# A Strassen-split GLA layer on one core: evictions and scan steps ranked first, TensorE in source order

## The chip, the cores and the metric

The kernel runs on one NeuronCore of a Trainium2 chip. The metric is the time of one execution in microseconds of the device. Each core has five engines that run their own instruction streams side by side: TensorE (PE, matrix products), VectorE (DVE), ScalarE (ACT), GpSimd (POOL) and SyncE (SP, here only a queue that issues DMAs). An engine takes its instructions strictly in the order of its stream, so one that waits holds up all behind it.

## The reference

The program computes one layer: an RMS norm, a gated linear attention mixer (GLA), a residual add, another norm, a feed-forward block with a causal convolution, a residual add and a final norm. The sequence has 2048 rows, the model 1024 columns, all float32. Cut to what matters:

```python
h = rmsnorm(x, mix_norm_w)
proj = h @ w_in                      # q, k, v, r, glr
log_a = log_sigmoid(glr @ w_gate2 + b_gate) / 16
g = cumsum(log_a, within chunks of 64);  g_end = g[:, :, -1]
k_dec = k * exp(g_end - g)
for each chunk:                      # lax.scan over 32 chunks
    state = state * exp(g_end) + k_dec.T @ v
    o = q @ state
y = (rms_normalize(o) * norm_w * silu(r)) @ w_out
x = x + y
h = rmsnorm(x, ffn_norm_w)
u = causal_dwconv(h @ w_up, conv_w, conv_b);  g, val = split(u)
x = x + (silu(g) * val) @ w_down
return rmsnorm(x, final_norm_w)
```

## The kernel before

**Products.** Every large matrix product is computed to float32 accuracy from two reduced parts of each operand: `split(hi, lo, src)` makes the rounded part on ACT (a cast, L193) and the rest on DVE (a subtraction, L194). `mm3p` (L181 to L187) then issues three matmuls for each of four k slices: L184 takes the low part of the weight, L185 the low part of the row operand, L186 both high parts. On top of that a Strassen-like scheme computes a pair of row tiles by a pair of column blocks with seven products instead of eight, in the order `PORD` = p1, p5, p6, p2, p7, p3, p4, so each product is 12 matmuls of 128x512. A product leaves its sum in an accumulator bank in PSUM; p6, p7 and p4 add onto p1's bank and p3 onto p5's. Between two products that share a bank the sum so far must be copied out: this is an eviction. It is `cp1`, `cp5`, `cp6` on ACT (L1211), `o11`, `o22`, `o12` on DVE (`out`, L1154), `o21` on ACT (L1227), in the last projection the additions to the residual `x1` on DVE (L1199), and in the feed-forward block `c1`, `c2` on ACT (`copied`, L1297). The next product on the bank waits for it.

**Phases.** Four phases R, A, B, Y of eight units j (one unit is a pair of row tiles e = 2j, d = 2j+1, in `unit`): R projects r and the gates, A and B project q, k, v of two heads each and run the scan, Y is the output projection with the residual add. Then U is the up projection of the feed-forward block with its convolution (`phase_u`, by row half s and column block f) and D the down projection. Each phase loads raw weights (`wr_...`) into a ring of slots, splits them into `w_...` and frees the slots; rows (`hr_...`) are loaded, split into `h_...`.

**Scan.** For each of 32 tiles n (16 of A, 16 of B) there are four steps, put in between the matmuls of the products by `scan_slot`: `scan_f` (decay `kd` and its split `kz`, transposes `pq`, gate rows `r` loaded by DMA and passed through silu on ACT, L714), `scan_k` (products `pk`, the running `state` on DVE, splits `sh` and `sl`), `scan_o` (products `po`, sums of squares, `og` on DVE, with `rstd` from POOL), `scan_x` (transposes `px` of `og`, copies `ot`). The table `SLOTS` says behind which k slice of a unit each one stands.

**Gates.** Block b of four row tiles has `sums(tt)`: two matmuls `pd` (L639) of the split logarithms `lh`, `ll`, an exponential on ACT into `e` (L640), and `totals`: four transposes `pe` of `e` (L631), whose last columns ACT copies to `dec` (L633). Blocks 0 to 2 fall in R, block 3 at the start of A. A table load (`ACT_TABLE_LOAD`) stands on ACT wherever exp and silu follow one another.

**Order.** The source issues the instructions in one long list, with delayed work (`later_do`) taken up at due times. `scan_b`, which runs in unit 0 of A after p3, calls `need` on all gates, so that in the source all of block 3's `pd` and `pe` stand ahead of p4 of that unit. A scheduler then sets the order on each engine: of the instructions that it takes as ready it picks the one earliest in the source. So before, PE too may run a later product ahead of a step that is not ready by the scheduler's reckoning.

## Time and profile before

| what | us |
|---|---|
| median of three runs (2118.75 to 2119.75) | 2118.95 |
| profiled execution | 2119.17 |
| its span | 2117.5 |
| PE busy in the span | 2049.1 |
| DVE, ACT, POOL busy | 1605.2, 1109.4, 672.5 |
| phases on PE: R, A, B, Y | to 220, 429, 643, 831 |
| phases on PE: U, D | to 1690, 2109 |

The span is what the trace covers; 1.67 us lie around it. A row of the profile gives a start in us from the span's start, a duration, engine, source line, output, inputs and shape; in square brackets is the idle time of the engine ahead of the row and what ended it. The trace's rows leave out the numbers in names (`mp_A` is any product's bank in A, `h_A_p` any row operand). "PEclk" is the granted clock of TensorE as a share of full speed.

### The profile page before, as it was taken

How to read it: one execution, taken by the hardware profiler on the slowest of the kernel's cores; microseconds unless marked ns; L12 is line 12 of the kernel's file. 1: busy time of each engine (PE TensorE's matmuls, PEld its weight loads, DVE VectorE, ACT ScalarE, POOL GpSimd, SP SyncE). 2: the span in 40 equal slices, each digit the busy share in tenths (PEclk: the TensorE clock that was granted, in tenths of full speed). 3: DMA queues.
4: the chain of work that ended last, by engine and by line, in shares of the span. 5: the costliest groups of instructions: out<-in, count | busy, mean ns of one | idle time of the engine just before them, and what ended most of it. 6: DMA issues, size and time to landing. Idle time of an engine off the chain costs nothing.

```text
span 2117.5 us, 28200 instructions
## 1 busy us (share of the span) xinstructions
PE 2049.1 (97%) x9700; PEld 1686.1 (80%) x9700; DVE 1605.2 (76%) x2109; ACT 1109.4 (52%) x2022; POOL 672.5 (32%) x595
## 2 busy tenths in 40 slices
PE   6999999999998998999999999999999999999998
PEld 4777778878886887888888887888888788888886
DVE  7766887888878646899898867898898956566564
ACT  5656755675665666655545545445454533233342
POOL 2110000000000002555464554666766433243310
PEclk9999999999999999999999999999999999999999
DMA  8866675577858888444545376545445684454462
GB/s 293 295 219 199 223 237 178 165 247 254 292 183 267 314 271 293 155 159 136 182 139 167 132 278 204 140 110 152 122 129 148 196 322 155 144 179 164 148 218 112
DMA packets 246512, 419.32 MB, mean 198 GB/s; under 512 B 22784, under 2 KB 91520, under 8 KB 246368
## 3 DMA queue, kind: packets, MB, share of 16 engines
q1 hardware_dynamic: 203200, 335.09, 46.5%
q10 hardware_dynamic: 36832, 70.89, 9.8%
q0 software_dynamic: 6336, 11.54, 3.5%
q8 instruction: 76, 1.25, 0.2%
q14 instruction: 68, 0.56, 0.1%
HBM read 278.50 MB, written 150.47 MB: 203 GB/s over the span
## 4 chain that ended last, share of the span: by engine, by line
PE 64%; DVE 13%; POOL 7%; issue 7%; DMA 7%; ACT 2%; SPq 0%; ACTq 0%; DVEq 0%; POOLq 0%
PE pd_p L184 7%; PE pd_p L186 7%; PE pd_p L185 7%; DVE t L1315 4%; PE ua L185 4%; PE ua L184 4%; PE ua L186 3%; POOL as_p L1344 3%; DVE uw_p L194 3%; PE mp_A L184 2%; PE mp_Y L184 2%; PE mp_Y L185 2%; PE mp_Y L186 2%; PE mp_A L185 2%; PE mp_A L186 2%
## 5 line engine op out<-in xcount | busy, mean ns | idle before, releaser
L184 PE MATMUL ua<-h_p,uw_p 128*128 128x512 f32 x704 | 276.9, 393 | 10.2 <-ACT c L1297 4.5
L185 PE MATMUL ua<-h_p,uw_p 128*128 128x512 f32 x704 | 276.0, 392 | 2.8 <-DVE var_d L226 2.8
L186 PE MATMUL ua<-h_p,uw_p 128*128 128x512 f32 x704 | 275.5, 391 | 0.0
L1315 DVE SCALAR_TENSOR_TENSOR t<-u,cw,t 128x1024 f32<-128x1024 f32 x176 | 265.6, 1512 | 8.5 <-ACT t L1313 7.8
L184 PE MATMUL pd_p<-dw_p,da 128*128 128x512 f32 x616 | 239.6, 389 | 0.0
L185 PE MATMUL pd_p<-dw_p,da 128*128 128x512 f32 x616 | 239.6, 389 | 0.0
L186 PE MATMUL pd_p<-dw_p,da 128*128 128x512 f32 x616 | 239.6, 389 | 0.0
L193 ACT CAST uw_p<-us 128x512 fp32r<-128x512 f32 x132 | 82.2, 622 | 198.8 <-POOL us L1277 138.3
L194 DVE TENSOR_TENSOR da<-da_p,da 128x512 fp32r<-128x512 f32 x154 | 118.9, 826 | 87.9 <-ACT da L193 87.9
L194 DVE TENSOR_TENSOR uw_p<-us,uw_p 128x512 fp32r<-128x512 f32 x132 | 153.3, 1166 | 42.4 <-ACT uw_p L193 37.7
L194 DVE TENSOR_TENSOR uw_p<-ur,uw_p 128x512 fp32r<-128x512 f32 x176 | 146.3, 860 | 28.1 <-ACT uw_p L193 28.1
L184 PEld LDWEIGHTS ua<-h_p,uw_p 128*128 128x128 f32 x704 | 133.0, 189 | 43.2 <-ACT c L1297 8.9
L193 ACT CAST da<-da_p 128x512 fp32r<-128x512 f32 x154 | 84.7, 618 | 150.4 <-PE pd_p L186 115.3
L185 PEld LDWEIGHTS ua<-h_p,uw_p 128*128 128x128 f32 x704 | 133.0, 189 | 30.6 <-DVE uw_p L194 3.4
L186 PEld LDWEIGHTS ua<-h_p,uw_p 128*128 128x128 f32 x704 | 133.2, 189 | 27.9
L760 POOL TENSOR_TENSOR rstd<-var,pair 128x2 f32<-128x2 f32 x32 | 22.7, 709 | 410.7 <-DVE var L759 410.7
L184 PE MATMUL uc<-h_p,uw_p 128*128 128x512 f32 x352 | 137.1, 390 | 1.2 <-DMA h_p<-hd_p 1.2
L186 PE MATMUL uc<-h_p,uw_p 128*128 128x512 f32 x352 | 137.0, 389 | 0.0
L185 PE MATMUL uc<-h_p,uw_p 128*128 128x512 f32 x352 | 136.9, 389 | 0.0
L1313 ACT ACTIVATE t<-u,cw 128x1024 f32<-128x1024 f32 x88 | 109.6, 1245 | 49.9 <-DVE u L1424 49.1
L186 PEld LDWEIGHTS pd_p<-dw_p,da 128*128 128x128 f32 x616 | 115.6, 188 | 24.1
L185 PEld LDWEIGHTS pd_p<-dw_p,da 128*128 128x128 f32 x616 | 115.6, 188 | 24.1
(263 smaller groups left out, 5287.3 us busy)
## 6 DMA issues: line engine op xcount, KB each, us to landing
ur<-in_ffn_w_up_dram SPq DMA_DIRECT2D x84, 512.0 KB, 5.2
da_p<-ad_p SPq DMA_DIRECT2D x154, 256.0 KB, 4.1
ad_p<-t SPq DMA_DIRECT2D x110, 256.0 KB, 3.1
ch<-in_ffn_w_down_dram SPq DMA_DIRECT2D x61, 256.0 KB, 4.9
hr_A_p<-h1d_p SPq DMA_DIRECT2D x56, 256.0 KB, 3.3
hr_B_p<-h1d_p SPq DMA_DIRECT2D x56, 256.0 KB, 3.2
hr_Y_p<-yd_p SPq DMA_DIRECT2D x56, 256.0 KB, 3.9
hd_p<-h2p_p ACTq DMA_DIRECT2D x56, 256.0 KB, 2.1
```

What stands on the lines that cost most here:

```text
L184: nc.tensor.matmul(ps_ap, ah, bl, start=(first and i == 0), stop=False, **kw)
L185: nc.tensor.matmul(ps_ap, al, bh, start=False, stop=False, **kw)
L186: nc.tensor.matmul(ps_ap, ah, bh, start=False, stop=(last and i == len(pairs) - 1), **kw)
L193: order["act"] = nc.scalar.copy(hi, src)
L194: nc.vector.tensor_sub(lo, src, f32(hi))
L760: nc.gpsimd.tensor_tensor(rstd, var, neghalf.to_broadcast([P, 2]), op=ALU.pow)
L1313: nc.scalar.activation(t, u[:, 2:2 + TS], AF.Identity, scale=cw[:, 2, c:c + 1], bias=cw[:, 3, c:c + 1])
L1315: nc.vector.scalar_tensor_tensor(t, u[:, k:k + TS], cw[:, k, c:c + 1], t, op0=ALU.mult, op1=ALU.add)
L1344: upool["ins"] = nc.gpsimd.tensor_add(av, last if x is None else x, y)
```

## The change

It does three things. `manual_schedule(engines={PE})` makes TensorE keep the order in which the source issues its instructions. `high_priority(600)` ranks the evictions, and `high_priority(400)` the steps `scan_o`, `scan_k` and `scan_x` (not `scan_f`), as though they stood that many places earlier in the source, on the engines that the scheduler still orders. `ROWS` is not used. No instruction's shape or data changes; ACT gets 14 table loads in place of 12.

```diff
+    ctx.enter_context(tc.manual_schedule(engines={mybir.EngineType.PE}))
...
+    def first(n):
+        return tc.high_priority(n)
+    EVICT, SCAN, ROWS = 600, 400, 200
...
         def scan_slot(m):
             if ps_ == "Y" and j < 2:
                 for fn, n in SLOTS_END.get(28 * j + m, ()):
-                    fn(2 * NTT + n)
+                    with ExitStack() if fn is scan_f else first(SCAN):
+                        fn(2 * NTT + n)
             if ps_ in "AB":
                 for fn, n in SLOTS.get(m, ()):
-                    fn(NTT * g + e + n)
+                    with ExitStack() if fn is scan_f else first(SCAN):
+                        fn(NTT * g + e + n)
...
-            nc.vector.scalar_tensor_tensor(t, src, rs[:, t_:t_ + 1], other, op0=ALU.mult, op1=ALU.add)
+            with first(EVICT):
+                nc.vector.scalar_tensor_tensor(t, src, rs[:, t_:t_ + 1], other, op0=ALU.mult, op1=ALU.add)
...
-                    add(xt[:, cs], xt[:, cs], a)
+                    with first(EVICT):
+                        add(xt[:, cs], xt[:, cs], a)
...
-                nc.scalar.activation(keep[o], a, AF.Identity, scale=rs[:, t_:t_ + 1])
+                with first(EVICT):
+                    nc.scalar.activation(keep[o], a, AF.Identity, scale=rs[:, t_:t_ + 1])
...
-                    nc.scalar.activation(o21, a, AF.Identity, scale=rs[:, e:e + 1])
+                    with first(EVICT):
+                        nc.scalar.activation(o21, a, AF.Identity, scale=rs[:, e:e + 1])
...
-            nc.scalar.copy(t, pa)
+            with first(EVICT):
+                nc.scalar.copy(t, pa)
```

Most rows keep their order. Behind the first blocks of U, and in all of D, the streams are the same up to a few rows; R differs by a few evictions that stand one cast earlier. The differences are at the start of A, in single rows through A and B, where one phase passes to the next, and at the end of Y. The numbers behind the names below are the program's own buffers; source lines move by up to 13 between the two files.

**PE at the start of A.** Before, the third transpose of block 3's gates (`pe_14`) and the last sums (`pd_3_3`) stand inside p5 of unit 1:

```order
L184 MATMUL mp5_A_1_2936<-w_A_p5_2474,h_A1_p5_2878 128x512
L631 MATMUL pe_14_2840<-ident_485,e_3_2_2674 128x128 x4
L639 MATMUL pd_3_3_2846<-ll_3_3_2837,later_555 128x512
L639 MATMUL pd_3_3_2846<-lh_3_3_2836,later_555 128x512
L185 MATMUL mp5_A_1_2936<-w_A_p5_2474,h_A1_p5_2878 128x512
```

Now all of them follow one another behind p3 of unit 0, and p4 of unit 0 (the bank `mp1_A_0`) comes after:

```order
L193 MATMUL mp5_A_0_2666<-w_A_p3_2720,h_A0_p3_2730 128x512
L638 MATMUL pe_13_2827<-ident_487,e_3_1_2650 128x128 x4
L646 MATMUL pd_3_2_2833<-ll_3_2_2819,later_557 128x512
L646 MATMUL pd_3_2_2833<-lh_3_2_2818,later_557 128x512
L638 MATMUL pe_14_2842<-ident_487,e_3_2_2676 128x128 x4
L646 MATMUL pd_3_3_2848<-ll_3_3_2839,later_557 128x512
L646 MATMUL pd_3_3_2848<-lh_3_3_2838,later_557 128x512
L638 MATMUL pe_15_2853<-ident_487,e_3_3_2681 128x128 x4
L191 MATMUL mp1_A_0_2631<-w_A_p4_2748,h_A0_p4_2761 128x512
```

All of p4 of unit 0, p1 of unit 1 and seven matmuls of p5 of unit 1 have moved from between `pe_12` and `pe_15` to behind `pe_15`.

**ACT at the start of A.** Before, from the first silu of gate rows (`r_0`) to the last exponential of block 3 (`e_3_3`):

```order
L714 ACT_TABLE_LOAD
L714 ACTIVATE r_0_2908<-r_0_2908 128x512
L633 COPY dec_494<-pe_13_2825 128x4x2
L640 ACT_TABLE_LOAD
L640 ACTIVATE e_3_2_2674<-pd_3_2_2831 128x512
L687 ACTIVATE vh_0_0_2893<-mp1_A_0_2629,rs_497 128x512
L193 CAST h_A1_p6_2913<-hr_A1_p6_2791 128x512
L633 COPY dec_494<-pe_14_2840 128x4x2
L1211 ACTIVATE cp1_A_1_2929<-mp1_A_1_2916,rs_497 128x512
L640 ACTIVATE e_3_3_2679<-pd_3_3_2846 128x512
```

Now:

```order
L721 ACT_TABLE_LOAD
L721 ACTIVATE r_0_2910<-r_0_2910 128x512
L640 COPY dec_496<-pe_13_2827 128x4x2
L647 ACT_TABLE_LOAD
L647 ACTIVATE e_3_2_2676<-pd_3_2_2833 128x512
L200 CAST h_A1_p6_2915<-hr_A1_p6_2793 128x512
L721 ACT_TABLE_LOAD
L721 ACTIVATE r_1_3023<-r_1_3023 128x512
L640 COPY dec_496<-pe_14_2842 128x4x2
L647 ACT_TABLE_LOAD
L647 ACTIVATE e_3_3_2681<-pd_3_3_2848 128x512
```

The silu of `r_1` has moved ahead of the last exponential, with a table load for each of the two.

**DVE where B passes to Y.** Before, the split of the raw weight `wr_Y_10` stands ahead of the gated rows `og_29`:

```order
L194 TENSOR_TENSOR w_Y_p7_7457<-wr_Y_9_7373,w_Y_p7_7457 128x1024
L194 TENSOR_TENSOR w_Y_p3_7520<-wr_Y_10_7415,w_Y_p3_7520 128x1024
L759 TENSOR_SCALAR var_29_7543<-ssq_29_7542 128x2
L739 SCALAR_TENSOR_TENSOR state_1_5368<-state_1_5368,dec_494,pk_30_0_7551 128x256
L763 SCALAR_TENSOR_TENSOR og_29_7541<-po_29_7528,rstd_29_7544,r_29_7322 128x256 x2
```

Now `og_29`, the state and `sl_30_0` stand ahead of it:

```order
L770 SCALAR_TENSOR_TENSOR og_29_7543<-po_29_7530,rstd_29_7546,r_29_7324 128x256 x2
L709 SCALAR_TENSOR_TENSOR kd_31_7650<-E_1_15_7446,pair_492,o12_B_7_7444 128x256
L746 SCALAR_TENSOR_TENSOR state_1_5370<-state_1_5370,dec_496,pk_30_0_7553 128x256 x2
L718 SCALAR_TENSOR_TENSOR q1_0_2869<-pq_30_7490,q0_0_2868 128x2x64
L201 TENSOR_TENSOR h_Y0_p6_7502<-hr_Y0_p6_7367,h_Y0_p6_7502 128x512
L201 TENSOR_TENSOR w_Y_p7_7459<-wr_Y_9_7375,w_Y_p7_7459 128x1024
L201 TENSOR_TENSOR sl_30_0_7570<-state_1_5370,sh_30_0_7569 128x512
L718 SCALAR_TENSOR_TENSOR q1_0_2869<-pq_30_7490,q0_0_2868 128x2x64
L746 SCALAR_TENSOR_TENSOR state_1_5370<-state_1_5370,dec_496,pk_30_1_7554 128x256 x2
L201 TENSOR_TENSOR w_Y_p3_7522<-wr_Y_10_7417,w_Y_p3_7522 128x1024
```

The weight split moved behind five steps of the scan. On PE, p6 of unit 0 of Y stood behind `px_29`, `pq_31` and four matmuls of p2; now it stands ahead of them. On DVE at the same place and where A passes to B, the low part of p4's rows in unit 7 (`h_A7_p4`, `h_B7_p4`) moved behind `og`, `o12` and `sl` and one or two weight splits.

In A's unit 3, ACT now has the eviction `cp6` ahead of the silu of `r_5`, and in unit 5 likewise ahead of `r_9`. At the end of Y, the transposes `pt_d12` stand ahead of p5 of unit 7 (before: behind six of its matmuls), and the split of U's first weight (`uw_0_0_p1`) on DVE stands behind `var_d14` (before: ahead of it).

## The prediction

> **What bounds the kernel now.** I read the busy times first, then PE's waits by what ended them, then PE by phase, and then the places of the largest waits instruction by instruction.

> ```profile
> span 2117.5 us, 28200 instructions
> PE 2049.1 (97%) x9700; PEld 1686.1 (80%) x9700; DVE 1605.2 (76%) x2109; ACT 1109.4 (52%) x2022; POOL 672.5 (32%) x595
> ```

> PE bounds the kernel: 97% busy. All that an order can win is PE's idle time, 2117.5 - 2049.1 = 68 us by this row, and the change leaves PE's work as it is. What an order can lose has no such limit.

> ```profile
> PE m_R L184 <- ACT h_R L193: 14.7, 1, 14.7
> PE px L771 <- DVE og L763: 7.0, 3, 4.9
> PE pe L631 <- ACT e L640: 5.2, 3, 2.7
> PE ua L184 <- ACT c L1297: 4.5, 5, 1.2
> PE mp_A L184 <- ACT cp_A L1211: 2.7, 3, 1.9
> PE mp_B L185 <- DVE h_B_p L194: 2.0, 2, 1.8
> ```

> These are PE's waits: the sum in us, how often, the longest. The 14.7 us are the start, before the first product's rows are split, and stay. The evictions `c` of U (4.5 us) and the gates in R (most of the 5.2) stay too, since the rows in U behind its first blocks and the `pd` and `pe` rows in R have kept their places. What the change can reach of these waits is `og` (7.0), `cp_A` (2.7) and a few like `h_B`: a dozen us at most.

> ```profile
> 220.00:429.00 209.00, 204.68 (x1102) 168.31 (x1101) 164.65 (x307) 130.51 (x275) 9.46 (x17) 0.99 0.62 201
> 429.00:642.60 213.60, 208.28 (x1154) 173.04 (x1153) 178.97 (x347) 137.90 (x306) 11.86 (x17) 0.99 0.73 245
> 642.60:831.00 188.40, 176.86 (x864) 145.80 (x863) 118.96 (x198) 118.21 (x258) 17.10 (x22) 0.99 0.84 290
> 142.00:146.00 4.00, 4.00 (x27) 3.30 (x26) 2.62 (x5) 1.89 (x5) 0.00 (x0) 1.00 0.92 260
> 309.00:312.00 3.00, 2.18 (x13) 1.56 (x11) 3.00 (x6) 0.13 (x1) 0.00 (x0) 1.00 0.90 311
> 314.00:317.00 3.00, 3.00 (x8) 2.32 (x8) 2.87 (x6) 1.55 (x5) 0.00 (x0) 0.50 0.54 217
> ```

> Stretches of time, with length, PE's busy time first, and near the end the granted clock. In A (220 to 429) PE is idle for 4.3 us, in B 5.3, in Y 11.5. The last two rows show a second price of a wait: around 309 to 312 the clock is full, and after the wait that ends at 313.13 (below) it is 0.50 from 314 to 317, where only eight matmuls run.

> **The change, part by part.**

> *Start of A.* In before, PE fills the time between block 3's gate steps with products:

> ```profile
> 240.31 0.66 PE L631 MATMUL pe<-ident,e 128*128 128x128 f32 x4
> 248.82 0.48 PE L639 MATMUL pd<-ll,later 128*128 128x512 f32 x1
> 250.76 0.60 PE L631 MATMUL pe<-ident,e 128*128 128x128 f32 x4
> 240.31:250.76 10.45, 7.72 (x32) 5.74 (x31) 2.16 (x3) 1.40 (x2) 1.00 0.49 164
> ```

> The first row is `pe_12`, the third `pe_15`; the last is that stretch with the products of A alone: they take 7.72 us of it. In the new order p4, p1 and seven matmuls of p5, 31 in all, come behind `pe_15`, and nine of p3 come in between. So PE now waits for the chain pd, exp on ACT, pe, four times over. Its links on ACT:

> ```profile
> 240.16 0.61 ACT L193 CAST lh<-e 128x512 fp32r<-128x512 f32 x1
> 243.84 0.61 ACT L193 CAST lh<-e 128x512 fp32r<-128x512 f32 x1
> 244.47 1.28 ACT L714 ACT_TABLE_LOAD   x1
> 245.76 0.63 ACT L714 ACTIVATE r<-r 128x512 f32<-128x512 f32 x1
> 247.76 0.60 ACT L640 ACTIVATE e<-pd 128x512 f32<-128x512 f32 x1
> ```

> I follow the new rows from 240.3, where `e_3_0` is done in before too (ACT works without a gap up to there, so little can come sooner). `lh_3_1` ends at 240.8, its low part on DVE about 0.7 later at 241.5, `pd_3_1` runs to about 242.1, the exp of `e_3_1` ends at 242.7. ACT then does `lh_3_3`, a table load, `r_0`, the copy of `pe_13`, a table load and the exp of `e_3_2`: 0.5 + 1.28 + 0.6 + 0.15 + 1.28 + 0.6 = 4.4, so 247.1. Meanwhile PE has nine matmuls of p3 (2.1), `pe_13` and `pd_3_2` (1.2), and is through at about 245.4: a wait of 1.7. Then `pe_14` and `pd_3_3` take 1.0 on PE, while ACT does `h_A1_p6`, a table load, `r_1`, a copy, a table load and the exp of `e_3_3`: 0.5 + 1.28 + 0.6 + 0.15 + 1.28 + 0.6 = 4.4. A wait of 3.4, and `pe_15` runs from 251.5 to 252.1. In before it ended at 251.4, with 31 matmuls more behind it. At 7.72 for 32 these are 7.5 us: a loss of 0.7 + 7.5 = 8.2, and with the two short waits that ACT's new order makes ahead of it (a row split that stands behind evictions) I take **+8.5**. Bounds: 6.5, if ACT reaches `e_3_0` a cast or two (0.6 each) sooner and a copy overlaps, and 11, if the load of `r_1` or a low part on DVE comes late by two splits of 1.2.

> [...]

> *Clock.*

> ```profile
> 311.87 0.63 ACT L714 ACTIVATE r<-r 128x512 f32<-128x512 f32 x1 [3.25 <-DMA r<-rd]
> 312.40 0.67 ACT L1211 ACTIVATE cp_A<-mp_A,rs 128x512 f32<-128x512 f32 x1
> 313.13 0.51 PE L184 MATMUL mp_A<-w_A_p,h_A_p 128*128 128x512 f32 x1 [1.95 <-ACT cp_A L1211]
> 313.13:317.73 4.60, 4.60 (x13) 0.63 0.51 205
> ```

> After a wait of 1.95 us the 12 matmuls of p7 take 4.6 us; at 7.72 for 32 they would take 2.9. So a wait of about 2 us can cost 1.7 us more behind it. The wait of 3.4 ahead of `pe_15` does the same to p4: **+1.7** (0 to 3.4, if the two earlier waits also bring one).

> *A, steady.* The rows above are also the gain: the eviction `cp6` of unit 3 stood on ACT behind the silu of `r_5`, which waited for its DMA until 311.87. Now it stands ahead of it, so 1.95 and the 1.7 of clock go. The same change of places in unit 5 takes away the second of the three `cp_A` waits: all three sum to 2.7, this one and a short one 0.8, of which I take 0.6. Together **-4.3** (bounds -5 and -2, if something else is late within the 1.95: DVE has no gap from 309 to 312).

> *A to B.*

> ```profile
> 423.48 0.68 DVE L194 TENSOR_TENSOR h_A_p<-hr_A_p,h_A_p 128x512 fp32r<-128x512 f32 x1
> 426.39 0.75 DVE L1154 SCALAR_TENSOR_TENSOR o_A<-mp_A,rs,cp_A 128x512 f32<-128x512 f32 x1 [1.40 <-PE mp_A L186]
> 426.42 0.39 PE L185 MATMUL mp_A<-w_A_p,h_A_p 128*128 128x512 f32 x1
> ```

> The low part `h_A7_p4` was done at 424.2, two us before p4's second matmul needs it at 426.42. Now it stands behind `o12`, which starts at 426.39 since it needs the end of p3, and `sl_13_0` (a 128x512 split, 0.7): 426.4 + 0.75 + 0.7 + 0.7 = 428.5, so p4 waits 2.1 us where it waited for nothing. Some of that is given back, since the split of `h_B0_p5` that PE waits for in B's first unit (the 1.8 above) has DVE's work ahead of it done by then, but the weight splits of 1.2 that moved in front of `kz` make a new wait of about that size. I take **+2** (0 to 4).

> *B to Y.*

> ```profile
> 655.04 2.36 DVE L194 TENSOR_TENSOR w_Y_p<-wr_Y,w_Y_p 128x1024 fp32r<-128x1024 f32 x2
> 657.43 0.33 SPq L404 DMA_DIRECT2D x<-in_x_dram  x1
> 658.89 0.69 PE L771 MATMUL px<-ident,og 128*128 128x128 f32 x2 [4.91 <-DVE og L763]
> 662.14 0.69 DVE L1199 TENSOR_TENSOR x<-x,mp_Y 128x512 f32<-128x512 f32 x1 [0.93 <-DMA x<-in_x_dram]
> 662.88 0.50 PE L184 MATMUL mp_Y<-w_Y_p,h_Y_p 128*128 128x512 f32 x1 [0.70 <-DVE x L1199]
> ```

> Here PE waits 4.9 us for `og_29`, which stands behind two weight splits (the first row). The change moves `og_29` ahead of them, so this wait for `og` goes. What is late next is the residual row `x1_0`: its DMA goes out at 657.43, as soon as the split of `wr_Y_10` (second of the first row's two) has freed its slot, and lands at 662.14, 4.7 later; p1's addition on it must be done before p6 may write the bank. In the new order that split stands behind `sl_30_0` (0.7), a state step (0.5) and `og_29` (0.9) too: 2.1 later. So the addition ends near 665 instead of 662.9, and PE, which now meets p6 first, has `px_29`, `pq_31` and four matmuls of p2 (from 658.89 to the wait before 662.88, 3.3 us, some 2.3 at full clock) still to do behind it: 2.1 + 2.3 = 4.4. With the late low part of p4 in unit 7, as at A to B, I take **+5** (2 to 9). A half clock after the wait is in both.

> *Y to U.*

> ```profile
> 810.42 0.48 PE L184 MATMUL mp_Y<-w_Y_p,h_Y_p 128*128 128x512 f32 x1
> 812.01 0.77 PE L840 MATMUL pt_d<-ident,h 128*128 128x128 f32 x5
> 834.24 0.68 DVE L194 TENSOR_TENSOR uw_p<-ur,uw_p 128x512 fp32r<-128x512 f32 x1
> 834.97 0.79 PE L185 MATMUL ua<-h_p,uw_p 128*128 128x512 f32 x1 [2.77 <-DVE var_d L226]
> 838.31 0.15 DVE L226 TENSOR_SCALAR var_d<-ssq_d 128x1 f32<-128x1 f32 x1 [2.73 <-ACT h L224]
> ```

> `pt_d12` can start at 812.0, when its row is normalized. Six matmuls of p5 bridged the time from 810.4; now they come after: about +1.4. The first product of U goes on at 834.97, after the split that ends at 834.92. This split now stands behind `var_d14`, which came at 838.31 and needs the square of row 14, itself brought forward on ACT by about two instructions of 1.1: near 836.5 instead, +1.9. Together **+3.3** (1.4 to 5).

> *R, U, D.* One cast less ahead of an eviction in R: -0.3. PE has no new wait there, and behind U's first blocks nothing moves: 0.

> **Sum:** 8.5 + 1.7 - 4.3 + 2 + 5 + 3.3 - 0.3 = +15.9. The profiled execution took 2119.17, 0.2 above the median of the runs, so 2135.

> **The rivals.** A difference of 0.2%, about 4.2 us, is what a measurement of this kernel can tell from no change.

> *Slower by more, through the clock.* Each new wait of about 2 us (ahead of `pe_14`, p4 of A7 and of B7, and the first splits of U) brings a half-clock stretch of its own like the one at 314: four times 1.7 added, 2142. For it speaks the row with 0.50 after 1.95 us; against it, that the wait of 2.7 us for `pe`, which ends at 141.2 in R, is followed by a full clock (1.00 from 142 to 146). [...]

> *No change.* The start of A loses only its bound of 6.5, and the passages between phases win as much as they lose, because DVE and ACT, which set them, do the same work in either order: 6.5 - 4.3 + 0 + 0 + 1.4 = +3.6, 2123 at most. For it speaks that the passages' waits are DVE's by the list of waits. Against it: the product matmuls at the start of A leave PE with nothing else.

> *Faster.* One mechanism: the scan's steps that now rank first run so early that PE never meets a wait on `og` or an eviction, at B to Y above all. The 4.9 us there go whole, if `x1_0` is there when p6 wants it. It decides if the slot of `wr_Y_10` is freed before 655, five us ahead of p6 in the new order; then B to Y gives -4.9 - 1.7 (its half clock), and with A's start at its lower bound and the other passages at 0: 6.5 - 4.3 - 6.6 = -4.4, 2115. The new order, with the split of `wr_Y_10` behind `og_29`, speaks against it.

> **How the numbers follow.** The forecast (2126 to 2139) has a chance of 0.58; slower by more through the clock or a longer wait for `x1_0`, 0.27; within 0.2% 0.09; faster 0.06. So slower by over 0.2% has 0.85. The range leaves out the fastest cases and the worst: 2121 to 2150, with the upper bounds of A's start (+2.5), the clock (+7) and B to Y (+4) above the forecast.

> **What would show it.** In the changed kernel: a wait of `pe` for the exponential in A of 5 us or more, with 14 table loads on ACT; no `cp_A` wait of 1.9; no wait of `px` for `og` of 4.9, and in its place one of p6 for `x1` of over 5 us; a wait of `pt_d` for `h` of 1.4. Busy time of PE the same but for the clock. The forecast is wrong if the waits of `pe` in A stay under 3 us, or if PE's idle time in B and Y falls.

## The result: 1.7% slower, about twice the loss that was forecast

The changed kernel takes 2154.97 us (median of four runs, 2154.43 to 2157.54) against 2119.35 for the kernel before (four runs, 2118.75 to 2121.88): ratio 1.0168, 95% interval 1.0153 to 1.0184. Forecast was 2135, within 2121 to 2150: the direction came true, the size did not, and the time lies outside the range. The profiled execution of the changed kernel took 2155.22, its span is 35.8 us longer.

First the page's head of the changed kernel, to be read against the same two rows of before:

```profile
span 2153.3 us, 28198 instructions
PE 2060.1 (96%) x9700; PEld 1693.8 (79%) x9700; DVE 1602.1 (74%) x2109; ACT 1113.1 (52%) x2024; POOL 673.7 (31%) x595
```

PE has the same 9700 matmuls and is busy 11.0 us longer (2060.1 - 2049.1): the same work at a lower clock (mean 0.986 over the span, 0.994 before). The other 24.8 us of the 35.8 are idle time of PE (93.2 now, 2153.3 - 2060.1; 68.4 before). The stretches of phases A, B and Y (length, PE busy first; the granted clock third from the end) of the changed kernel, which answer to the three that the prediction shows of before:

```profile
223.00:444.00 221.00, 208.70 (x1103) 171.56 (x1103) 169.63 (x315) 135.18 (x281) 10.28 (x18) 0.96 0.62 197
444.00:667.00 223.00, 209.47 (x1145) 172.61 (x1144) 176.10 (x342) 137.35 (x302) 12.46 (x17) 0.98 0.69 231
667.00:865.00 198.00, 180.73 (x873) 149.38 (x871) 118.75 (x195) 118.38 (x256) 17.09 (x21) 0.97 0.81 275
```

Idle time of PE rises from 4.3 to 12.3 in A, from 5.3 to 13.5 in B and from 11.5 to 17.3 in Y, and the clock falls in all three. PE's waits by what ended them (sum, times, longest), after:

```profile
PE pe L638 <- ACT e L647: 10.4, 6, 2.4
PE mp_Y L191 <- DVE x L1210: 8.7, 1, 8.7
PE ua L191 <- ACT uw_p L200: 8.3, 1, 8.3
PE mp_B L192 <- DVE h_B_p L201: 5.8, 4, 3.2
PE mp_A L192 <- DVE h_A_p L201: 4.6, 2, 3.7
PE px L778 <- DVE og L770: 3.2, 2, 2.1
```

`cp_A` is gone from the top of the list and `og` is down from 7.0 to 3.2. In their place stand the gates (`e`), the residual `x`, and low parts of row splits (`h_A_p`, `h_B_p`), all of them things that now come later on ACT or DVE. The 8.3 for `uw_p` is no new kind: it is the 3.1 and 2.8 that stood there in two waits before, joined, and 2.4 more.

How far the changed kernel lags behind before, by the end of a product's last matmul in the two traces (lag grows where time is lost). At each of these points both kernels have run the same matmuls, so what a stretch gains or loses splits into PE's idle time and PE's busy time, and the second is the clock:

| stretch | lag at its end, us | gained or lost | of it idle | of it clock | forecast |
|---|---|---|---|---|---|
| R (p4 of its unit 7) | 3.0 | +3.0 | -0.4 | +3.4 | -0.3 |
| start of A (p6 of unit 1) | 13.4 | +10.4 | +6.9 | +3.5 | +8.5 and +1.7 of clock |
| A (p3 of unit 7) | 8.7 | -4.7 | -2.6 | -2.1 | -4.3 (1.7 of it clock) |
| A to B (p4 of B's unit 0) | 15.7 | +7.0 | +4.1 | +2.9 | +2 |
| B (p3 of unit 7) | 23.7 | +8.1 | +5.3 | +2.7 | none |
| B to Y (p5 of unit 1) | 30.2 | +6.5 | +4.6 | +1.9 | +5 |
| Y (p2 of unit 4) | 32.3 | +2.1 | +1.9 | +0.2 | none |
| Y to U (first products) | 35.7 | +3.4 | +3.7 | -0.3 | +3.3 |
| U and D | 35.5 | -0.2 | +0.9 | -1.1 | 0 |

The passage A to B, B and Y lose 17.2 together where 2 was forecast: 15.2 of the miss of 19.6 (35.5 - 15.9). Put the other way, 11.0 of the 35.5 are clock, where the sum had 1.7 lost and 1.7 gained.

R makes 3.3 of the miss, and nothing shows that it is the change's. PE's idle time there is 0.4 shorter, as forecast; the rest is two half-clock stretches of 3.4 us (from 69.27 and from 144.36), half of which is lost, that the trace of before does not have. The kernel with three buffers for `r` (below), whose instructions in R stand in before's order on PE, ACT and DVE, has two of them as well, and its R is 3.3 longer. Five kernels that share the changed kernel's order in R on these three engines reach A at 221.8 to 228.9 (the changed kernel at 223.1, before at 220.0), with 6.8 to 17.1 us of half clock. Two such waits, one with half clock behind it and one without, are set side by side further down, with the clock.

### The profile page after: what moved, and what is told of

The parts are those of the page before. It is cut to its first block, busy times and chain, and to the rows that moved or that the text cites. A ratio compares the mean times of both kernels' runs of the same rounds, so it can differ in the third digit from the quotient of the medians.

```text
span 2153.3 us, 28198 instructions
## 1 busy us (share of the span) xinstructions
PE 2060.1 (96%) x9700; PEld 1693.8 (79%) x9700; DVE 1602.1 (74%) x2109; ACT 1113.1 (52%) x2024; POOL 673.7 (31%) x595
## 4 chain that ended last, share of the span: by engine, by line
PE 62%; DVE 14%; DMA 7%; issue 7%; POOL 6%; ACT 3%; SPq 0%; ACTq 0%; DVEq 0%; POOLq 0%
PE pd_p L192 6%; PE pd_p L193 6%; PE pd_p L191 6%; DVE t L1329 4%; PE ua L191 3%; PE ua L192 3%; PE ua L193 3%; DVE uw_p L201 2%; POOL as_p L1358 2%; PE mp_A L191 2%; PE mp_Y L191 2%; PE mp_A L192 2%; PE mp_A L193 2%; PE mp_Y L193 2%; PE mp_Y L192 2%
## 5 line engine op out<-in xcount | busy, mean ns | idle before, releaser
L193 PE MATMUL ua<-h_p,uw_p 128*128 128x512 f32 x704 | 274.7, 390 | 0.0
L193 PE MATMUL pd_p<-dw_p,da 128*128 128x512 f32 x616 | 239.6, 389 | 0.0
L193 PEld LDWEIGHTS ua<-h_p,uw_p 128*128 128x128 f32 x704 | 132.6, 188 | 27.8
L193 PE MATMUL uc<-h_p,uw_p 128*128 128x512 f32 x352 | 137.0, 389 | 0.0
```

What stands on the lines that cost most here:

```text
L193: nc.tensor.matmul(ps_ap, ah, bh, start=False, stop=(last and i == len(pairs) - 1), **kw)
```

## Experiments

Ratios below are to the kernel before, run on the same chip, with 95% intervals. Steps by stretch are worked out as in the table above.

### The order of TensorE alone

```diff
 # in the kernel before
+    ctx.enter_context(tc.manual_schedule(engines={mybir.EngineType.PE}))
```

> TensorE keeps the source's order, no step is ranked up. Theory S (the source order is what costs): about 2150 us, with the start of A as in the changed kernel (+10 us between p6 of unit 0 and p5 of unit 1), the 1.9 us wait for cp6 in unit 3 of A back, and at least as much waiting for px in B. Rival R (the ranks are what costs, by pushing row and weight splits back): about 2130, only the start of A is lost, and A to B and B cost nothing.

Measured: 2140.06, ratio 1.0093 [1.0070, 1.0116]. So some 20 us of the 36 come from PE's order alone, between what the two theories gave. In its trace R is 6.0 longer, 5.0 of it clock; then the start of A loses 13.0, A gains 2.2, A to B gains 1.4, B is unchanged, B to Y loses 3.9, Y 1.0 and Y to U 1.1. The gates of block 3 are the largest place. Its waits:

```profile
PE pe L632 <- ACT e L641: 8.5, 4, 3.3
PE mp_A L185 <- ACT cp_A L1212: 4.7, 3, 2.7
```

One of the three waits for `cp_A`, 2.7, stands at the start of A; the other two, 2.0 together, are those in A of before. So the end of these waits in the changed kernel is the ranks' doing, and the order's own gain in A is mostly clock (1.7 of 2.2). At A to B and in B the order by itself costs nothing: the 15 us lost there in the changed kernel need the ranks.

### The ranks alone

The changed kernel without the `manual_schedule` line.

> The ranks alone; the scheduler orders TensorE as before. Theory S: about 2112 us, 7 faster than before: the wait for cp6 in A and half of the wait for og_29 are gone and nothing is lost at the start of A. Rival R: 2135 or more, slower than before, since p4 of unit 7 waits for its rows whatever TensorE's order.

Measured: 2221.76, ratio 1.0480 [1.0452, 1.0508], the worst of the three. It is slower, as the rival said, but not by the rival's waits: PE's idle time is only 4.3 us above before's (2218.2 - 2145.5 = 72.7). What rises is its busy time:

```profile
PE 2145.5 (97%) x9700; PEld 1733.1 (78%) x9700; DVE 1609.0 (73%) x2109; ACT 1112.0 (50%) x2022; POOL 669.6 (30%) x595
```

The scheduler, free on PE, pulls `scan_k` of one tile up to `scan_o` of another and issues their matmuls by turns. PE's rows there, and two such steps in before:

```profile
319.84 0.38 PE L738 MATMUL pk<-vl,kz 64*128 64x256 f32 x1
320.15 0.38 PE L191 MATMUL po<-sh,q 128*128 128x256 f32 x1
320.46 0.38 PE L738 MATMUL pk<-vl,kz 64*128 64x256 f32 x1
```

```profile
422.77 0.28 PE L185 MATMUL po<-sh,q 128*128 128x256 f32 x1
422.89 0.28 PE L186 MATMUL po<-sh,q 128*128 128x256 f32 x1
423.10 0.39 PE L732 MATMUL pk<-vl,kz 64*128 64x256 f32 x2
```

By the starts, 0.31 us from one matmul to the next where the 64-row and 128-row forms alternate, 0.12 where `po` stands in a block. In that block of before the `pk` matmuls start in pairs, 3 to 4 ns apart, with 0.12 from pair to pair; in the step that begins at 319.84 here, 10 of 12 start singly. Summed from each start to the next, `po` and `pk` take 155 us here and 82 in before: 73 of the 101 us between the two traces. I read this as the price of the alternation and tested it by itself:

### Two scan steps by turns, in the order of the changed kernel

```diff
+    def scan_ok(no, nk):
+        a_, b_ = [], []
...
+        for x, y in zip(a_, b_):
+            for args, kw in (x, y):
+                nc.tensor.matmul(*args, **kw)
```

Here `a_` and `b_` hold the 12 matmuls of each step. `scan_o` of a tile and `scan_k` of the next are issued together, 29 pairs of steps.

> The changed kernel, with the 12 matmuls of scan_o (128 rows of the array) and the 12 of scan_k for the next tile (64 rows) issued by turns in place of one block after the other, as the scheduler put them when it applied the ranks to TensorE too. Theory A (changing from one shape to the other on TensorE is what costs in the run with the ranks alone): each pair takes 7 to 8 us in place of 2.6, 28 pairs or so, and the time rises by about 100, to 2250 or more. Rival: the alternation is harmless, the ranks lose their 100 us elsewhere, and the time stays within 10 us of 2155.

Measured: 2392.81, ratio 1.1282 [1.1253, 1.1312], 238 us above the changed kernel where about 100 was expected, since the clock falls as well (mean 0.938, 0.986 in the changed kernel). PE's idle time is 88 us, no more than in the changed kernel: all of the loss is busy time. Two neighbouring stretches of this kernel (PE busy first, clock third from the end):

```profile
346.00:349.00 3.00, 3.00 (x11) 1.78 (x10) 0.00 (x0) 0.00 (x0) 0.00 (x0) 0.98 0.98 357
349.00:352.00 3.00, 3.00 (x7) 1.71 (x7) 1.20 (x3) 0.69 (x4) 0.00 (x0) 0.50 0.01 2
```

PE counts as busy without a gap, and still only 11 matmuls run in 3 us and the clock behind them is 0.50. So the alternation costs by itself, and the source order on PE is what makes the ranks bearable: it keeps the blocks together.

### One rank at a time

```diff
-    EVICT, SCAN, ROWS = 600, 400, 200
+    EVICT, SCAN, ROWS = 600, 0, 200      # first kernel
+    EVICT, SCAN, ROWS = 0, 400, 200      # second kernel
```

> Source order on TensorE, only the evictions ranked up (the scan's rank is 0). Theory S: about 2146 us, 4 less than source order alone, by the eviction of unit 3 in A. Rival R: p4 of unit 7 (A and B) has its rows in time again, 2130 or less.

> Source order on TensorE, only the scan's steps ranked up (the evictions' rank is 0). Theory S: about 2154 us, near source order alone, some less waiting for px. Rival R: as slow as the changed kernel or slower, 2155 to 2160, with p4 of unit 7 in A waiting 2 us or more for h_A7_p4 and the wait for cp6 in A back.

Measured: 2139.88, 1.0091 [1.0062, 1.0120] with the evictions ranked, 2145.61, 1.0121 [1.0097, 1.0145] with the scan's steps ranked. Against the order alone (1.0093) the first is nothing, where 4 us less was expected, and the second about 6 us, with intervals that overlap and below what either theory gave; both together are 1.0168. In both traces PE's waits for `cp6` in units 3 and 5 of A are gone, and unit 3 gains 3.8 as in the changed kernel, so either rank alone brings this. Their largest other waits, first the kernel with evictions ranked, then the one with the scan ranked:

```profile
PE px L778 <- DVE og L770: 16.3, 13, 4.4
```

```profile
PE mp_Y L191 <- DVE x L1210: 4.1, 1, 4.1
PE pk L739 <- DVE vl L695: 3.6, 1, 3.6
```

What ranks lower is what PE waits for: `og` in the one, the residual row and the split of the values in the other.

### The two ranks exchanged

In B of the changed kernel, DVE's rows between units 3 and 4, and last PE's:

```profile
557.72 1.22 DVE L302 TENSOR_TENSOR wm_Y<-wm_Y,wm_Y 128x1024 f32<-128x1024 f32 x1
...
558.86 0.74 DVE L1164 SCALAR_TENSOR_TENSOR o_B<-mp_B,rs,cp_B 128x512 f32<-128x512 f32 x1
...
560.12 0.48 DVE L770 SCALAR_TENSOR_TENSOR og<-po,rstd,r 128x256 f32<-128x256 f32 x1
...
560.74 0.63 PE L778 MATMUL px<-ident,og 128*128 128x128 f32 x2 [2.05 <-DVE og L770]
```

`og` needs `rstd` from POOL, which takes the variance from DVE and is not back at 557.72 (its row on POOL runs from 557.96 to 559.49). The sum `wm_Y` fills that gap, the eviction `o_B` (600) then goes ahead of `og` (400), and a split `sl` (559.52) as well; PE, held to the source, waits 2.05 for `og`. In before the same `og` waits 0.87 for `rstd` and the sum comes after it:

```profile
536.19 0.88 DVE L763 SCALAR_TENSOR_TENSOR og<-po,rstd,r 128x256 f32<-128x256 f32 x2 [0.87 <-POOL rstd L760]
...
538.09 1.22 DVE L295 TENSOR_TENSOR wm_Y<-wm_Y,wm_Y 128x1024 f32<-128x1024 f32 x1
...
538.51 0.38 PE L771 MATMUL px<-ident,og 128*128 128x128 f32 x2
```

The transposes `px` stand at the same place of PE's order before and after; only DVE's order moved. So the rank of the evictions over `og` should be what costs here, and exchanging the ranks should give it back:

```diff
-    EVICT, SCAN, ROWS = 600, 400, 200
+    EVICT, SCAN, ROWS = 400, 600, 200
```

> The changed kernel with the two ranks exchanged: evictions 400, scan steps 600. TensorE's order is the same. Theory P (in B, the evictions o12 and the sums that fill the wait for rstd stand ahead of og on VectorE, and TensorE waits for px): og_20 now stands ahead of o12_B_3, the wait for px_20 falls from 2.05 to under 0.7 us, B from unit 1 to unit 6 loses 3 us or less in place of 7.8, and the time is 2146 to 2151. Rival K (any rank makes B lose): px_20 or another wait in B of over 1.5 us stays and the time is 2153 or more.

Measured: 2143.55, ratio 1.0126 [1.0103, 1.0149]; its interval lies below that of the changed kernel, and the time below what was expected. B loses 3.3 instead of 8.1 (from unit 1 to unit 6, 2.7 instead of 7.8), A to B 3.8 instead of 7.0. At the same place:

```profile
552.38 0.88 DVE L770 SCALAR_TENSOR_TENSOR og<-po,rstd,r 128x256 f32<-128x256 f32 x2 [0.58 <-POOL rstd L767]
...
553.01 0.74 PE L778 MATMUL px<-ident,og 128*128 128x128 f32 x4 [0.46 <-DVE og L770]
...
553.77 0.74 DVE L1164 SCALAR_TENSOR_TENSOR o_B<-mp_B,rs,cp_B 128x512 f32<-128x512 f32 x1
```

`og` is again ahead of the eviction, and PE's wait falls to 0.46. About 9 of the ranks' 16 us hang on this one relation (1.0168 - 1.0126, times 2119; the 16 are 1.0168 - 1.0093). The exchange also moves each rank against the work that has none, which was not tried apart. The runs with one rank agree with the reading: B loses 6.0 with the evictions ranked alone, 1.1 with the scan's steps ranked alone.

### Moving the sums of Y

```diff
-        if ps_ in "AB" and j in (2, 4):
+        if (ps_, j) in (("A", 2), ("A", 4), ("B", 3), ("B", 5)):
             make_sums(nxt, j // 2 - 1)
```

> The changed kernel, with the sums of Y's raw weights made in units 3 and 5 of B in place of 2 and 4 (A is left as it is). Theory M (these sums on DVE, 1.2 us each and their scalings on ACT stand between the scan's steps that TensorE meets in source order, and make B's waits for px_16, px_20 and cp of unit 3): these waits go, and waits of the same kind appear one unit later, 7 us in all as before; the time stays within 4 us of 2155. Rival K (the ranks make these waits by themselves): px_16 and px_20 still wait for 1 us or more.

Measured: 2155.18, ratio 1.0178 [1.0163, 1.0194], as expected. The wait moved with the sums, to the next even tile:

```profile
586.31 0.41 PE L778 MATMUL px<-ident,og 128*128 128x128 f32 x2 [2.06 <-DVE og L770]
```

From unit 1 to unit 6, B loses 7.7, and 7.8 without the move. The sums fix where `og` is late, not how much it costs. Another wait for `og` in B, 1.15 us at 506.72, stayed where it was (506.25 in the changed kernel): that one is not the sums', and for it the rival holds.

### Row splits ranked highest

```diff
     def split_row(ps_, j, o, src):
         t = w_pair(f"h_{ps_}{j}_{o}")
-        split(t[:, 0, :], t[:, 1, :], src)
+        with first(800):
+            split(t[:, 0, :], t[:, 1, :], src)
```

> The changed kernel, with the splits of row operands ranked above evictions and scan steps (800). Theory D (the ranks put evictions and scan steps ahead of row splits that the next product needs): the waits for h_A7_p4 (3.7), h_B7_p4 (3.2) and B's first rows (5.8 in all by now) go, and the time falls by 6 to 12, to 2143 to 2149. Rival W (something is always last: with rows first, weight splits or evictions come late by as much): the rows' waits go, others of the same size come, and the time stays at 2152 to 2158.

Measured: 2152.09, ratio 1.0169 [1.0136, 1.0202], no gain, as the rival said. The waits of `mp_A` and `mp_B` for low parts are gone. A to B falls to +1.3, and units 1 to 6 of B to +0.5. Others took their place: A loses 0.7 instead of gaining 4.7, B's unit 7 loses 4.8 and Y 5.9:

```profile
PE px L779 <- DVE og L771: 6.3, 4, 3.4
PE pk L740 <- ACT kz L200: 5.2, 1, 5.2
```

### The gates of block 3 later

```diff
             if ps_ in "AB":
+                late = ps_ == "A" and j == 1
+                if late and m == 8:
+                    scan_b()
+                    scan_f(0)
+                if late and m == 12:
+                    with first(SCAN):
+                        scan_k(0)
                 for fn, n in SLOTS.get(m, ()):
+                    if ps_ == "A" and NTT * g + e + n == 0 and (j == 0 or m == 7):
+                        continue
...
-                    if j == 0 and g == 0:
-                        scan_b()
```

> The changed kernel, but the scan is opened (and all gates asked for) behind p5 of unit 1 of A in place of behind p3 of unit 0, with the first scan_f and scan_k just behind it; so in the source block 3's pd and pe stand 12 matmuls apart, inside p3, p4, p1 and p5. Theory S (TensorE meets the gate chain with nothing else to do): the 12.7 us that A's start loses shrink to 3 or less, and the time falls by 8 to 11, to about 2145. Rival L (the two more table loads and ACT's new order make the loss, wherever the steps stand): waits for the exponentials of over 4 us stay, and the time stays within 4 us of 2155.

Measured: 2150.68, ratio 1.0148 [1.0124, 1.0171]. At the start of A one wait for an exponential is left, in place of waits of 1.35, 2.15 and 2.44:

```profile
PE pe L638 <- ACT e L647: 1.4, 1, 1.4
```

From p6 of unit 0 to p4 of unit 2 the loss falls from 12.6 to 4.9. The time fell by 4.3, where 8 to 11 was expected, with overlapping intervals. R of its profiled execution is 8.9 longer than before's, with 17.1 us of half clock, so the trace shows the gain of the stage, and the times only agree in sign.

### Keeping TensorE busy in the gates' waits

```diff
             pe = aux_ps(f"pe_{t}")
+            for _ in range({12: 8, 14: 14, 15: 20}.get(t, 0)):
+                nc.tensor.matmul(pe[:, :P], rp["later"], rp["later"], start=True, stop=True)
```

Extra matmuls, of no use to the result, fill three of the waits.

> The changed kernel, with idle TensorE time filled: 8, 14 and 20 matmuls of 128x128 on constants, whose result is overwritten, stand ahead of the transposes pe_12, pe_14 and pe_15. Nothing else waits for less. Theory C (half clock behind these waits costs on top of them): the half-clock stretch of 10 us at the start of A goes, and with it 3 to 5 us of the 12.7 lost there; the whole time falls by as much, near 2151. Rival N (the clock is not set by these waits): the same half-clock stretch, and the time rises by 0 to 2.

The start of A, first in the changed kernel and then with the filling (clock third from the end):

```profile
256.00:260.00 4.00, 4.00 (x11) 3.03 (x11) 0.91 (x2) 0.48 (x2) 0.00 (x0) 0.50 0.68 214
```

```profile
255.00:259.00 4.00, 4.00 (x21) 3.25 (x20) 2.83 (x6) 1.77 (x4) 0.00 (x0) 1.00 0.91 299
```

The half clock is gone, and in 4 us 21 matmuls run instead of 11. From p6 of unit 0 to p6 of unit 1 the stage takes 10.0 instead of 12.7 above before, a gain of 2.7 where 3 to 5 was expected. The whole did not change by what the times can tell: 2154.89, ratio 1.0172 [1.0149, 1.0195].

### A third buffer for the gate rows

```diff
-        r = scan[n]["r"] = sp["a"].tile([P, 512], F32, tag="r", name=f"r_{n}", bufs=2)
+        r = scan[n]["r"] = sp["a"].tile([P, 512], F32, tag="r", name=f"r_{n}", bufs=3)
```

In the kernel before: an earlier load of `r` instead of a rank for `cp6`.

> The kernel before, with three buffers in place of two for the gate rows r, so that their DMA goes out a tile earlier and the silu no longer holds cp6 behind it. Theory E (the wait of 1.9 us for cp6 in unit 3 and its half clock, and 0.6 in unit 5, are the silu's wait for its DMA): both waits go, 2 to 4 us faster, about 2115. Rival: another instruction on ACT is late in their place, within 1 us of before.

Measured: 2113.38 (11 runs) against 2118.63 (15), ratio 0.9982 [0.9973, 0.9990], some 4 us faster than before by the ratio, as expected; but not by the way expected:

```profile
315.88 0.63 ACT L714 ACTIVATE r<-r 128x512 f32<-128x512 f32 x1 [3.49 <-DMA r<-rd]
...
317.13 0.51 PE L184 MATMUL mp_A<-w_A_p,h_A_p 128*128 128x512 f32 x1 [2.61 <-ACT cp_A L1211]
```

The scheduler put the next tile's silu where `r_5` had stood, and PE waits for `cp6` 2.61, no less than before (1.95). In the trace, of an execution of 2117.0, the gains lie at A to B (-3.1) and in U and D (-3.3), with one half-clock stretch less in each. In U it is the one that stands at 1672.2 in before, behind a wait of 2.48 for `c`; here the same wait is 2.18 and no half clock follows. So what the third buffer itself does for the time stays open.

### Source order without its costliest place

The order alone, with the later gates and three buffers for `r`, no ranks.

> Source order on TensorE, no ranks, with the scan opened later as in e5_gates and three buffers for r as in e9_r3. Theory S: of the 20 us that source order alone loses, 8 to 11 come back at the start of A and 2 to 4 in A, and 6 to 8 stay where B passes to Y and Y to U: 2126 to 2131. Rival: the waits reappear elsewhere, 2136 or more.

Measured: 2128.09, ratio 1.0047 [1.0034, 1.0061], the time that was expected, but only in part by the shares expected. The gates and the buffer, not tried apart on this base, take back about 10 us of the order's 20 by the ratios. In the trace the start of A loses 3.5 instead of 13.0, as expected; A gains 0.3, less than the order alone (2.2) and not 2 to 4 more; and B to Y, where with Y to U 6 to 8 were to stay, gains 2.4. Behind the start, `px` for `og` (13.0 in 8 waits) is the largest wait that is left. No version with the source order reached the kernel before.

## Why the prediction was wrong

**Right in the mechanism.** The start of A: 10.4 measured, 10.2 forecast, by the chain that was followed row by row. PE waits for the third and fourth exponential (2.15 and 2.44; forecast 1.7 and 3.4), with the silu and two table loads between them on ACT (rows of both engines, in order of time):

```profile
250.34 1.12 PE L638 MATMUL pe<-ident,e 128*128 128x128 f32 x4 [2.15 <-ACT e L647]
...
250.82 1.28 ACT L721 ACT_TABLE_LOAD   x1
252.11 0.63 ACT L721 ACTIVATE r<-r 128x512 f32<-128x512 f32 x1
...
252.81 1.28 ACT L647 ACT_TABLE_LOAD   x1
254.11 0.60 ACT L647 ACTIVATE e<-pd 128x512 f32<-128x512 f32 x1
...
254.76 1.12 PE L638 MATMUL pe<-ident,e 128*128 128x128 f32 x4 [2.44 <-ACT e L647]
```

That the number fits to 0.2 is luck. Idle time makes 6.9 (8.5 forecast) and the clock 3.5 (1.7 forecast); and from p6 of unit 0 on, where the chain lies, the loss is 12.7, with 2.3 won back ahead of it that the sum did not have. Each of the two table loads takes 1.28 and the next instruction starts 0.01 behind it, as in before (load at 244.47, silu at 245.76).

The waits for the evictions `cp6` in A (-4.7, forecast -4.3) are gone: 2.6 of idle time, and 2.1 of clock for the 1.7 of the sum. (The row behind that 1.7 counts 13 matmuls, not 12.) The residual row at B to Y (+6.5, forecast +5): its wait is 8.7. Its DMA goes out at 684.08, 26.6 later than before's; with B's lag of 23.7 taken off that is 2.9, and 2.1 was worked out. Y to U (+3.4, forecast 3.3), with a wait of `pt_d` of 1.35 where 1.4 was forecast. The rival of no change falls, since the passages lose; the faster one too, since the slot of `wr_Y_10` is freed late and `x1` with it.

**Wrong: the term "A to B, +2".** Measured 7.0. I let `o12` start at 426.39 as in before and added two splits behind it. DVE and PE there, after:

```profile
432.75 1.23 DVE L201 TENSOR_TENSOR w_B_p<-wr_B,w_B_p 128x1024 fp32r<-128x1024 f32 x1 [0.90 <-ACT w_B_p L200]
...
436.10 0.88 DVE L770 SCALAR_TENSOR_TENSOR og<-po,rstd,r 128x256 f32<-128x256 f32 x2 [0.68 <-POOL rstd L767]
...
436.90 0.74 DVE L1164 SCALAR_TENSOR_TENSOR o_A<-mp_A,rs,cp_A 128x512 f32<-128x512 f32 x1
...
438.15 0.69 DVE L201 TENSOR_TENSOR h_A_p<-hr_A_p,h_A_p 128x512 fp32r<-128x512 f32 x1
...
438.89 0.79 PE L192 MATMUL mp_A<-w_A_p,h_A_p 128*128 128x512 f32 x1 [3.65 <-DVE h_A_p L201]
```

Ahead of `o12` DVE itself waits 0.90 for a cast and 0.68 for `rstd`. With the lag of 8.7 taken off, `o12` starts at 428.2, not 426.39, and PE waits 3.65 where 2.1 was worked out. The rest is clock:

```profile
439.00:444.00 5.00, 5.00 (x13) 3.83 (x14) 3.56 (x6) 0.62 (x1) 0.00 (x0) 0.50 0.72 222
```

Half clock runs for 6.8 us from about 438 and 3.4 more from about 455; none was in this term. By the table 4.1 of the 7.0 are idle time and 2.9 clock. I looked at what moved behind what, and not at DVE's own waits in the new order.

**Wrong: no term for the steady parts of B and Y.** B lost 8.1, Y 2.1, 7.2 of it idle time. The prediction costed A and the passages between phases and put B and Y at nothing without a reason. On PE the steps of B did keep their places, but on DVE `og` fell behind an eviction, and PE, whose order is fixed, stood still until it came. The exchange of the ranks shows that this relation costs most of B's share; that PE would have had something else to run in a free order is argued, since the run with the ranks alone loses by something else. For Y the loss was only read from a row (`pt_d` waits 2.05 for its row at 728.25) and not tried.

**Wrong: the clock at 1.7, taken back in A.** It cost 11.0 net, 7.6 without R. The rival "slower by more, through the clock" had the right direction with 2142, and its size was still too small. Half-clock stretches of 3.4 to 10.2 us stand in R, at the start of A, at A to B, in B, at B to Y and at Y to U: 54.6 us in all, 20.5 in before. The half clock at the start of A stands among waits of 1.35, 2.15 and 2.44, and filling them, with the order kept, takes it away (0.50 from 256 to 260; in the filled kernel 1.00 from 255 to 259). The two runs with alternating matmuls show it with no idle gap at all: the ranks alone at 0.51 from 325.2 to 327.5 with PE busy for 2.30 of 2.30 us, the steps by turns at 0.50 from 349 to 352 with 3.00 of 3.00.

The prediction held the wait of 2.7 at 141.2 in before, with a full clock behind it, against this rival. The traces show how it differs from one that has half clock behind it. In the traces of before and after, all 30 changes of the granted clock behind the first one stand a whole number of 3.41 us steps from it. In these two traces half clock went with long idle time of PE within one such step (its length less PE's busy time); the counts are in the last section. Before's wait for `pe` that ends at 141.15 is split by a step's end; the changed kernel's shorter one (2.20, to 142.95) falls nearly whole into one step:

```profile
136.18:139.60 3.42, 2.22 (x11) 1.48 (x9) 0.35 (x1) 0.00 (x0) 0.37 (x1) 1.00 0.51 183
139.60:143.01 3.41, 1.86 (x13) 1.56 (x14) 2.04 (x4) 1.62 (x3) 0.00 (x0) 1.00 0.52 130
```

```profile
140.95:144.36 3.41, 1.41 (x8) 1.25 (x9) 1.58 (x3) 1.62 (x3) 0.00 (x0) 1.00 0.34 98
144.36:147.77 3.41, 3.41 (x15) 2.76 (x14) 2.07 (x4) 1.89 (x5) 0.00 (x0) 0.50 0.90 261
```

Idle for 1.20 and 1.55 within its steps, before stays at full clock; idle for 2.00, the changed kernel goes to 0.50. Where a wait falls on these steps shifts with everything ahead of it. So I take it that one half-clock stretch more or less (1.7 us lost, half of 3.41) can come or go without being an effect of the change; no run tried this apart.

**R, -0.3:** +3.0 measured. As told above its idle time came out as forecast, and the 3.4 of clock are such stretches behind waits that before has as well.

## What to carry to other kernels

A rank is a relation: whatever ranks lower is what the engine with a fixed order waits for, so look at each pair of chains that meet on one engine, and let the one that the busiest engine needs first win (`og` over the evictions here). Where the order of the bounding engine is fixed, it has nothing else to run in a wait, so a step of another engine that becomes late is paid for, and places where nothing moved on the bounding engine have to be costed too. Such a change is best tried in halves and with the ranks exchanged before it is judged.
